# SiLU as one ScalarE function, a sum of weight blocks in place, and memory keys normalised from PSUM, in a four-layer decoder trunk

## The chip, the cores and the metric

The kernel runs on one core of a Trainium2 chip. The core has TensorE (PE; its weight loads are shown apart as PEld), VectorE (DVE), ScalarE (ACT), GpSimd (POOL) and SyncE (SP), which here issues DMAs. The metric is device time in microseconds of one execution of the whole kernel; less is better.

## What is computed

A decoder trunk of four layers over 256 tokens of width 1024, all in float32. Each layer is half a SwiGLU, a token mixer with a memory attention beside it, and another half SwiGLU:

```python
def swiglu(x, wg, wu, wd):
    return (jax.nn.silu(x @ wg) * (x @ wu)) @ wd          # d_ff = 2816

for i in range(4):
    h = rms_norm(x, ffn_norm[i, 0]); x = x + 0.5 * swiglu(h, ...)
    h = rms_norm(x, mix_norm[i])
    y_mix, q_mem = (retention, dsa, nsa)[i % 3](h)        # layers 0 and 3: retention
    y_mem = memory_attention(q_mem, mem, ...)
    x = x + concatenate([y_mix, y_mem]) @ w_out[i]
    h = rms_norm(x, ffn_norm[i, 1]); x = x + 0.5 * swiglu(h, ...)

def memory_attention(q_raw, mem, norm_g, w_kv, qn, kn):   # 256 memory tokens, 4 heads of 64
    k, v = split(rms_norm(mem, norm_g) @ w_kv)
    k = rms_norm(k per head, kn); q = rms_norm(q_raw per head, qn)
    return softmax(q @ k.T / 8) @ v
```

## The kernel before

The 256 tokens are two blocks `t` of 128. Weights come from HBM as units of two blocks of 1 MB (128 x 2048 floats), read in one order by SP's queue (`load`, line 184) into three buffers called `raw`; a load can go out only when its buffer has been read for the last time, and the loads keep their order.

**Split weights.** Each product is made as three matmuls, so each quarter of a unit (128 x 1024) is split first: ACT copies it into `hi` (type F32R), DVE subtracts that from the source into `lo` (lines 281, 282). There are nine buffers of each. `mm3` (lines 309 to 311) multiplies hi, lo and hi by the split activations `sh`, `sl`. The splits are handed out by `tick`, once or twice per projection of 24 matmuls (`project`).

**An FFN** (`ffn`) walks through eleven gate-and-up units and six units of down rows in the order FFN_ORDER. A gate-and-up projection gives a PSUM bank `pg` of 128 x 512 (256 gate, 256 up), from a ring of two banks shared with all other projections. Line 1265 takes tanh of half the gate on ACT, line 1266 makes (tanh + 1) times the gate on DVE, line 1271 multiplies by the up half and by the square of the row's norm factor r into `h`; the bank is free then. Two ticks later PE transposes h (line 1279), and ACT and DVE split the result (1280, 1281). Since this h holds twice the SiLU, line 1298 adds the down projection to x with 0.25. The factors r, r/2 (`rh`) and r*r (`r2`) come from `norm_stats` by four small POOL instructions.

**Joint units.** Gate-and-up units 4 with 5 and 8 with 9 of each FFN (16 joint units in all) are multiplied by a scheme with seven products in place of eight (`joint`, lines 491 to 493). It needs sums of weight blocks: `t1` = b12 + b11 comes by a load and an adding DMA on POOL's queue (line 229) into two tiles of the kind `sum` (a ring of nine tiles with the tag a4); `t2` and `t4` are made by DVE in place over t1 (line 250); `t3` is t1 minus b11 by DVE (line 247), into two more a4 tiles. Each of the seven is then split as above (lines 253, 254). The three other raw blocks b11, b22, b21 fill the three `raw` buffers; the buffer of b11 is the first to be free, and the first load of down rows behind the joint unit goes into it.

**The memory's keys** (`mem_kv`, twice per layer, for all four layers): a projection into `pmkv`; ACT copies the keys, scaled by the row's factor, into `mk0` and the values into V; POOL squares mk0, DVE sums per head, POOL makes the power -1/2 (`rsqrt`, lines 392 and 394) and multiplies mk0 by it; PE transposes the result (line 691) into `mkT`. The helper `head_sq` (line 554), used for queries, squares on ACT straight from PSUM and sums on DVE.

The order of each engine's instructions is not that of the code: the framework lays it out from dependencies and its own durations, per engine, except in the opening (`in_order`). Exp is used in the mixers alone (lines 601 and 1165), all of a block's mixer work being flushed ahead of its output projection.

Of the kernel before, what the change touches and what calls it, by code (L numbers as in the profile page):

```python
# [11 lines left out]
AF = mybir.ActivationFunctionType  # L12
OP = mybir.AluOpType
AX = mybir.AxisListType
# [66 lines left out]
class Net:  # L81
# [155 lines left out]
    def split_joint(self, u):  # L237
        nc = self.nc
        raw, parts = self.raw.pop(u), self.parts[u]
        parts.update({n: [] for n in ("b11", "t1", "t2", "t3", "b21", "t4", "b22")})  # L240
        half = lambda n, q: raw[n][:, 1024 * q:1024 * q + 1024] if n[0] == "b" else raw[n][q]

        def quarter(name, src, q, plus):
            x = half(src, q)
            if name == "t3":
                raw.setdefault("t3", []).append(self.t4([128, 1024], "sum"))
                nc.vector.tensor_sub(raw["t3"][q], x, half("b11", q))
                x = raw["t3"][q]
            elif plus:
                nc.vector.tensor_add(x, x, half(plus, q))  # L250
            hi = self.wp.tile([128, 1024], F32R, name="hi", tag="hi", bufs=HALVES)
            lo = self.wp.tile([128, 1024], F32R, name="lo", tag="lo", bufs=HALVES)
            nc.scalar.activation(hi, x, AF.Copy)  # L253
            nc.vector.tensor_sub(lo, x, hi.bitcast(F32))  # L254
            parts[name].append((hi, lo))

        for name, src, plus in (("b11", "b11", None), ("t1", "t1", None), ("t2", "t1", "b22"), ("t3", "t1", None),
                                ("b21", "b21", None), ("t4", "t1", "b21"), ("b22", "b22", None)):
            for q in range(2):
                self.splits.append((u, lambda name=name, src=src, q=q, plus=plus: quarter(name, src, q, plus)))  # L260
# [395 lines left out]
    def mem_kv(self, i, um, uw):  # L656
        nc = self.nc
        mh, ml = zip(*self.parts[um])
        kT = self.t2([128, 2, 256], "mkT")
        V = self.t2([128, 2, 4, 65], "mV")  # L660
        self.memkv[i] = kT, V
        nc.gpsimd.memset(V[:, :, :, 64:65], 1.0)

        class Stationary:
            def __init__(self, tiles, c):
                self.t, self.c = [x.rearrange("p (k m) -> p k m", k=4) for x in tiles], c

            def __getitem__(self, key):
                return self.t[key[1] // 4][:, key[1] % 4, self.c]

        for m in range(2):
            p = self.pB("pmkv")
            c = slice(m * 128, m * 128 + 128)
            self.project(p, (Stationary(mh, c), Stationary(ml, c)), uw)
            r = self.rmem[m]
            k0 = self.t1([128, 4, 64], "mk0")
            nc.scalar.activation(k0.rearrange("p h d -> p (h d)"), p[:, :256], AF.Copy, scale=r)
            nc.scalar.activation(V[:, m, :, :64], p[:, 256:].rearrange("p (h d) -> p h d", d=64),
                                 AF.Copy, scale=r)
            sq = self.t1([128, 4, 64], "mksq")  # L680
            nc.gpsimd.tensor_tensor(sq, k0, k0, op=OP.mult)
            ss = self.ts(4, "mss")
            nc.vector.tensor_reduce(ss, sq, axis=AX.X, op=OP.add)
            rk = self.rsqrt(ss, 4, 1.0 / 64, EPS, "mrk")
            k1 = self.t1([128, 4, 64], "mk1")
            nc.gpsimd.tensor_tensor(k1, k0, rk[:, :, None].to_broadcast([128, 4, 64]), op=OP.mult)

            def turn(k1=k1, c=c):
                pt = self.pC("pT")
                for j in range(2):  # L690
                    nc.tensor.transpose(pt[:, j], k1[:, 2 * j:2 * j + 2].rearrange("p h d -> p (h d)"), self.ident)
                nc.scalar.activation(kT[:, :, c], pt[:, :2], AF.Copy, scale=self.mqk[:, i:i + 1])

            self.later(WAIT["mkv"], turn, 2)
            self.tick()
# [548 lines left out]
    def ffn(self, t, g, st):  # L1244

        nc = self.nc
        H, acc, nd = {}, None, 0
        X = self.X[t]
        for kind, ui in FFN_ORDER:
            u = yield  # L1250
            if not H:
                s, r, rh, r2 = st["n"]
            if kind == "g":
                r_, rh_, r2_ = r, rh, r2
                if u == 0:
                    p = self.first[t]
                elif isinstance(u, tuple):
                    p, (_, r_, rh_, r2_) = u
                else:
                    p = self.pB("pg")  # L1260
                    self.project(p, s, u)
                if t and ui == 0:
                    self.sums()
                th = self.t1([128, 256], "th")
                nc.scalar.activation(th, p[:, :256], AF.Tanh, scale=rh_)  # L1265
                nc.vector.scalar_tensor_tensor(th, th, 1.0, p[:, :256], op0=OP.add, op1=OP.mult)  # L1266

                if ui % 2 == 0:
                    h = self.t2([128, 512], "h")
                hs = h[:, ui % 2 * 256:ui % 2 * 256 + 256]  # L1270
                nc.vector.scalar_tensor_tensor(hs, th, r2_, p[:, 256:], op0=OP.mult, op1=OP.mult)
                if ui % 2 or ui == 10:
                    n = 4 if ui % 2 else 2
                    hl = H[ui // 2] = [self.t2([128, 4, 128], f"hT{x}", F32R) for x in "hl"]

                    def turn(h=h, hl=hl, n=n):
                        c = self.pC("pT")
                        for k in range(n):
                            nc.tensor.transpose(c[:, k], h[:, k * 128:k * 128 + 128], self.ident)  # L1279
                        nc.scalar.activation(hl[0][:, :n], c[:, :n], AF.Copy)  # L1280
                        nc.vector.tensor_sub(hl[1][:, :n], c[:, :n], hl[0][:, :n].bitcast(F32))  # L1281

                    self.later(WAIT["h"], turn)
            else:
                pr = self.parts[u]
                if acc is None:
                    acc = self.pA("acc")
                nk = len(pr)
                for cb in range(2):
                    for k in range(nk):  # L1290
                        hl = H[ui]
                        wh, wl = pr[k]
                        o = cb * 512
                        self.mm3(acc[cb], hl[0][:, k], hl[1][:, k], wh[:, o:o + 512], wl[:, o:o + 512],
                                 nd == 0 and k == 0, nd == 5 and k == nk - 1)
                    if nd == 5:
                        xs = X[:, cb * 512:cb * 512 + 512]
                        nc.vector.scalar_tensor_tensor(xs, acc[cb], 0.25, xs, op0=OP.mult, op1=OP.add)
                        if g is None:
                            nc.scalar.dma_start(self.a["out"][t * 128:(t + 1) * 128, cb * 512:cb * 512 + 512], xs)  # L1300
                        else:
                            (self.norm_half if g >= 8 else self.norm_kept)(t, g, cb, st)
                    if cb == 0:
                        self.tick()
                nd += 1
        if g is not None:
            self.norm_stats(t, st)
# [303 lines left out]
```

## Time and profile before

| | us |
|---|---|
| median of 3 runs | 2041.11 (2036.3 to 2041.76) |
| the profiled execution, its own time | 2034.82 |
| its span, first to last instruction | 2033.0 |
| PE busy | 2004.1 (99%) |
| DVE busy | 1554.8 (76%) |
| ACT busy | 1114.5 (55%) |
| POOL busy | 198.5 (10%) |

The granted clock of TensorE is 0.998 of full speed over the span. In the page's groups and the lists by line, a row names line, engine, operation, output and inputs, shape and count, then busy microseconds in total, mean nanoseconds of one, idle time of that engine just before them and what ended it. Matmuls overlap: one shows 0.39 us although the next starts 0.23 us later.

### The profile page before, as it was taken

How to read it: one execution, taken by the hardware profiler on the slowest of the kernel's cores; microseconds unless marked ns; L12 is line 12 of the kernel's file. 1: busy time of each engine (PE TensorE's matmuls, PEld its weight loads, DVE VectorE, ACT ScalarE, POOL GpSimd, SP SyncE). 2: the span in 40 equal slices, each digit the busy share in tenths (PEclk: the TensorE clock that was granted, in tenths of full speed). 3: DMA queues.
4: the chain of work that ended last, by engine and by line, in shares of the span. 5: the costliest groups of instructions: out<-in, count | busy, mean ns of one | idle time of the engine just before them, and what ended most of it. 6: DMA issues, size and time to landing. Idle time of an engine off the chain costs nothing.

```text
span 2033.0 us, 25241 instructions
## 1 busy us (share of the span) xinstructions
PE 2004.1 (99%) x9486; PEld 1615.2 (79%) x9486; DVE 1554.8 (76%) x2241; ACT 1114.5 (55%) x1562; POOL 198.5 (10%) x317
## 2 busy tenths in 40 slices
PE   8999999999999999999999999999999999999999
PEld 6777777888888787888788788878888878778887
DVE  7877756888787787887788876668887878657875
ACT  5545555556555555655555554555555646545553
POOL 0000402000001022100000113220000000301000
PEclk9999999999999999999999999999999999999999
DMA  6656535565545533655556553135655566435553
GB/s 246 221 187 228 187 117 194 165 229 222 192 186 178 203 114 125 205 189 169 218 193 232 188 179 131 67 110 202 217 197 186 166 228 223 150 125 199 194 166 125
DMA packets 57770, 368.53 MB, mean 181 GB/s; under 512 B 6576, under 2 KB 6992, under 8 KB 18864
## 3 DMA queue, kind: packets, MB, share of 16 engines
q1 hardware_dynamic: 51696, 347.76, 46.3%
q0 software_dynamic: 4800, 17.19, 4.8%
q10 hardware_dynamic: 1152, 1.97, 0.3%
q8 instruction: 75, 1.23, 0.2%
q14 instruction: 47, 0.39, 0.1%
HBM read 365.84 MB, written 1.05 MB: 180 GB/s over the span
## 4 chain that ended last, share of the span: by engine, by line
PE 87%; DMA 5%; DVE 4%; ACT 1%; issue 1%; POOL 1%; SPq 0%; ACTq 0%; POOLq 0%; DVEq 0%
PE pg L309 8%; PE pg L311 8%; PE pg L310 8%; PE acc L310 8%; PE acc L311 8%; PE acc L309 8%; DMA sum<-gu 4%; PE pg L492 3%; PE pg L491 3%; PE pg L493 3%; PE p L309 3%; PE p L310 3%; PE p L311 3%; PE pT L1279 2%; PE pT L564 1%; PE po L309 1%
## 5 line engine op out<-in xcount | busy, mean ns | idle before, releaser
L282 DVE TENSOR_TENSOR lo<-raw,hi 128x1024 fp32r<-128x1024 f32 (+3 forms) x516 | 614.1, 1216 | 103.3 <-ACT hi L281 96.8
L281 ACT ACTIVATE hi<-raw 128x1024 fp32r<-128x1024 f32 (+3 forms) x516 | 527.3, 1046 | 187.0 <-PE pg L311 53.7
L309 PE MATMUL pg<-hi,sh 128*128 128x512 f32 x896 | 355.5, 397 | 4.5 <-ACT hi L1364 3.4
L310 PE MATMUL pg<-lo,sh 128*128 128x512 f32 x896 | 351.1, 392 | 0.7 <-DVE lo L1365 0.7
L311 PE MATMUL pg<-hi,sl 128*128 128x512 f32 x896 | 350.0, 391 | 0.0
L310 PE MATMUL acc<-lo,hTh 128*128 128x512 f32 x704 | 281.1, 403 | 0.5 <-DVE lo L282 0.3
L311 PE MATMUL acc<-hi,hTl 128*128 128x512 f32 x704 | 278.8, 400 | 0.0
L309 PE MATMUL acc<-hi,hTh 128*128 128x512 f32 x704 | 278.1, 399 | 0.0
L253 ACT ACTIVATE hi<-sum 128x1024 fp32r<-128x1024 f32 x128 | 132.3, 1058 | 166.8 <-PE acc L311 82.2
L309 PEld LDWEIGHTS pg<-hi,sh 128*128 128x128 f32 x896 | 168.5, 188 | 39.6 <-ACT hi L1364 4.8
L311 PEld LDWEIGHTS pg<-hi,sl 128*128 128x128 f32 x896 | 168.5, 188 | 35.5
L310 PEld LDWEIGHTS pg<-lo,sh 128*128 128x128 f32 x896 | 168.8, 188 | 35.1 <-DVE lo L1365 2.3
L254 DVE TENSOR_TENSOR lo<-sum,hi 128x1024 fp32r<-128x1024 f32 x128 | 154.4, 1227 | 42.0 <-ACT hi L253 39.9
L310 PEld LDWEIGHTS acc<-lo,hTh 128*128 128x128 f32 x704 | 132.7, 188 | 36.8 <-DVE lo L282 7.6
L1265 ACT ACTIVATE th<-pg,rh 128x256 f32<-128x256 f32 x128 | 60.3, 471 | 178.4 <-PE pg L311 173.0
L309 PEld LDWEIGHTS acc<-hi,hTh 128*128 128x128 f32 x704 | 132.9, 189 | 29.4 <-ACT hTh L1280 1.6
L311 PEld LDWEIGHTS acc<-hi,hTl 128*128 128x128 f32 x704 | 132.9, 189 | 26.1 <-DVE hTl L1281 0.2
L1266 DVE SCALAR_TENSOR_TENSOR th<-th,pg 128x256 f32<-128x256 f32 x128 | 53.5, 418 | 101.8 <-ACT th L1265 101.2
L254 DVE TENSOR_TENSOR lo<-raw,hi 128x1024 fp32r<-128x1024 f32 x96 | 114.6, 1223 | 16.5 <-ACT hi L253 16.3
L309 PE MATMUL p<-hi,sh 128*128 128x512 f32 (+4 forms) x320 | 125.2, 391 | 0.3 <-DVE dq_b L546 0.3
L311 PE MATMUL p<-hi,sl 128*128 128x512 f32 (+4 forms) x320 | 121.2, 379 | 0.0
L310 PE MATMUL p<-lo,sh 128*128 128x512 f32 (+4 forms) x320 | 120.9, 378 | 0.0
(345 smaller groups left out, 3180.1 us busy)
## 6 DMA issues: line engine op xcount, KB each, us to landing
raw<-gu SPq DMA_DIRECT2D x158, 1024.0 KB, 5.1
raw<-dn SPq DMA_DIRECT2D x88, 1024.0 KB, 4.8
raw<-ret SPq DMA_DIRECT2D x20, 1024.0 KB, 4.9
sum<-gu SPq DMA_DIRECT2D x32, 512.0 KB, 7.0
sum<-gu POOLq DMA_DIRECT2D x32, 512.0 KB, 9.5
raw<-wout SPq DMA_DIRECT2D x16, 1024.0 KB, 4.8
raw<-mkv SPq DMA_DIRECT2D x8, 1024.0 KB, 4.9
raw<-nsa SPq DMA_DIRECT2D x6, 1024.0 KB, 4.9
```

Source lines behind the costliest of these rows:

```text
L253: nc.scalar.activation(hi, x, AF.Copy)
L254: nc.vector.tensor_sub(lo, x, hi.bitcast(F32))
L281: nc.scalar.activation(hi, src, AF.Copy)
L282: nc.vector.tensor_sub(lo, src, hi.bitcast(F32))
L309: mm(out, ah, bh, start=start, stop=False)
L310: mm(out, ah, bl, start=False, stop=False)
L311: mm(out, al, bh, start=False, stop=stop)
L491: mm(bank, a[0][:, k], bh, start=first and k == 0, stop=False, skip_group_check=True)
L492: mm(bank, a[0][:, k], bl, start=False, stop=False, skip_group_check=True)
L493: mm(bank, a[1][:, k], bh, start=False, stop=k == 3, skip_group_check=True)
L1265: nc.scalar.activation(th, p[:, :256], AF.Tanh, scale=rh_)
L1266: nc.vector.scalar_tensor_tensor(th, th, 1.0, p[:, :256], op0=OP.add, op1=OP.mult)
```

## The change

Three edits. In the FFN, ACT's Tanh becomes Silu with the factor r, the DVE pass of line 1266 goes, the product with the up half takes r in place of r2, and x gets 0.5 in place of 0.25. In the joint units, t3 is written over the raw block b11 in place of two new tiles. In `mem_kv`, the scaled copy k0 goes; squares come from PSUM by `head_sq` on ACT; POOL multiplies the power by the row's factor (4 columns); and a DVE pass multiplies the keys from PSUM.

```diff
             if name == "t3":
-                raw.setdefault("t3", []).append(self.t4([128, 1024], "sum"))
-                nc.vector.tensor_sub(raw["t3"][q], x, half("b11", q))
-                x = raw["t3"][q]
+                nc.vector.tensor_sub(half("b11", q), x, half("b11", q))
+                x = half("b11", q)
...
             r = self.rmem[m]
-            k0 = self.t1([128, 4, 64], "mk0")
-            nc.scalar.activation(k0.rearrange("p h d -> p (h d)"), p[:, :256], AF.Copy, scale=r)
+
+            ss = self.head_sq(p[:, :256], 4, r, "mk")
             nc.scalar.activation(V[:, m, :, :64], p[:, 256:].rearrange("p (h d) -> p h d", d=64),
                                  AF.Copy, scale=r)
-            sq = self.t1([128, 4, 64], "mksq")
-            nc.gpsimd.tensor_tensor(sq, k0, k0, op=OP.mult)
-            ss = self.ts(4, "mss")
-            nc.vector.tensor_reduce(ss, sq, axis=AX.X, op=OP.add)
             rk = self.rsqrt(ss, 4, 1.0 / 64, EPS, "mrk")
+            rr = self.ts(4, "mrr")
+            nc.gpsimd.tensor_scalar(rr, rk, r, None, op0=OP.mult)
             k1 = self.t1([128, 4, 64], "mk1")
-            nc.gpsimd.tensor_tensor(k1, k0, rk[:, :, None].to_broadcast([128, 4, 64]), op=OP.mult)
+            nc.vector.tensor_mul(k1, p[:, :256].rearrange("p (h d) -> p h d", d=64),
+                                 rr[:, :, None].to_broadcast([128, 4, 64]))
...
-                nc.scalar.activation(th, p[:, :256], AF.Tanh, scale=rh_)
-                nc.vector.scalar_tensor_tensor(th, th, 1.0, p[:, :256], op0=OP.add, op1=OP.mult)
+                nc.scalar.activation(th, p[:, :256], AF.Silu, scale=r_)
...
-                nc.vector.scalar_tensor_tensor(hs, th, r2_, p[:, 256:], op0=OP.mult, op1=OP.mult)
+                nc.vector.scalar_tensor_tensor(hs, th, r_, p[:, 256:], op0=OP.mult, op1=OP.mult)
...
-                        nc.vector.scalar_tensor_tensor(xs, acc[cb], 0.25, xs, op0=OP.mult, op1=OP.add)
+                        nc.vector.scalar_tensor_tensor(xs, acc[cb], 0.5, xs, op0=OP.mult, op1=OP.add)
```

## Rows read from the trace of the kernel before

**Rows 1.** Page, part 1: busy time, share of the span, instructions of each engine.

```profile
PE 2004.1 (99%) x9486; PEld 1615.2 (79%) x9486; DVE 1554.8 (76%) x2241; ACT 1114.5 (55%) x1562; POOL 198.5 (10%) x317
```

**Rows 2.** Waits of PE: waiting line, releaser: us in total, times, longest.

```profile
PE pT L1279 <- DVE h L1271: 9.3, 6, 4.1
...
PE pT L691 <- POOL mk L686: 2.9, 3, 1.4
PE pT L564 <- ACT nsa_p L601: 2.0, 2, 1.2
```

**Rows 3.** Windows: stretch, us, busy of PE, PEld, DVE, ACT, POOL, clock, DMA.

```profile
69.96:73.37 3.41, 3.41 (x10) 2.68 (x9) 3.41 (x4) 3.01 (x6) 1.08 (x3) 0.50 0.00 0
73.40:100.00 26.60, 26.60 (x116) 21.47 (x115) 22.69 (x24) 15.96 (x18) 1.72 (x2) 1.00 0.50 180
```

**Rows 4.** Timeline at 940 us: start, us, instruction, [idle before, its releaser].

```profile
939.83 1.06 ACT L253 ACTIVATE hi<-sum 128x1024 fp32r<-128x1024 f32 x1 [2.22 <-DMA sum<-gu]
...
940.80 0.46 ACT L1265 ACTIVATE th<-pg,rh 128x256 f32<-128x256 f32 x1
...
941.29 0.42 DVE L1266 SCALAR_TENSOR_TENSOR th<-th,pg 128x256 f32<-128x256 f32 x1 [1.17 <-ACT th L1265]
...
941.63 1.22 DVE L254 TENSOR_TENSOR lo<-sum,hi 128x1024 fp32r<-128x1024 f32 x1
...
943.29 0.44 PE L1279 MATMUL pT<-ident,h 128*128 128x128 f32 x2 [0.84 <-DVE h L1271]
```

**Rows 5.** Timeline at 67 us, the longest wait for h.

```profile
67.71 0.41 DVE L1266 SCALAR_TENSOR_TENSOR th<-th,pg 128x256 f32<-128x256 f32 x1
...
69.71 0.49 PE L1279 MATMUL pT<-ident,h 128*128 128x128 f32 x2 [4.06 <-DVE h L1271]
```

**Rows 6.** Groups by line: shapes, count, busy us, mean ns, idle before.

```profile
L1265 ACT ACTIVATE th<-pg,rh 128x256 f32<-128x256 f32 x128 | 60.3, 471 | 178.4 <-PE pg L311 173.0 <-POOL rh L529 4.4
...
L1266 DVE SCALAR_TENSOR_TENSOR th<-th,pg 128x256 f32<-128x256 f32 x128 | 53.5, 418 | 101.8 <-ACT th L1265 101.2
...
L1266 DVE SCALAR_TENSOR_TENSOR th<-th,s 128x256 f32<-128x256 f32 x48 | 18.8, 419 | 0.0
...
L686 POOL TENSOR_TENSOR mk<-mk,mrk 128x256 f32<-128x256 f32 x8 | 7.0, 876 | 0.6
...
L681 POOL TENSOR_TENSOR mksq<-mk 128x256 f32<-128x256 f32 x8 | 6.2, 773 | 34.3 <-ACT mk L677 34.3
...
L847 POOL TENSOR_SCALAR nsc<-dq,rstd 128x6 f32<-128x6 f32 x4 | 1.6, 404 | 0.4
...
L1394 ACT ACT_TABLE_LOAD x1 | 1.3, 1283 | 5.6 <-DMA gains<-gains 5.6
```

**Rows 7.** Timeline of a joint unit at 395 us, and the page's row for down loads.

```profile
391.92 11.08 SPq L184 DMA_DIRECT2D raw<-dn  x2
...
394.57 3.50 DVE L254 TENSOR_TENSOR lo<-sum,hi 128x1024 fp32r<-128x1024 f32 x3 [1.58 <-ACT hi L253]
...
405.59 3.91 ACT L281 ACTIVATE hi<-raw 128x1024 fp32r<-128x1024 f32 x4
...
raw<-dn SPq DMA_DIRECT2D x88, 1024.0 KB, 4.8
```

**Rows 8.** Timeline in the NSA layer: its first Exp and PE behind it.

```profile
1252.41 1.85 ACT L601 ACTIVATE nsa_p<-nsa_s,nb,nsc 128x128 f32<-128x128 f32 x5 [1.82 <-DVE nb L598]
...
1252.92 0.33 PE L564 MATMUL pT<-ident,nsa_p 128*128 128x128 f32 x1 [0.81 <-ACT nsa_p L601]
```

**Rows 9.** Timeline of the opening: the first Tanh, and PE's wait for a bank.

```profile
25.84 0.47 ACT L1265 ACTIVATE th<-pg,rh 128x256 f32<-128x256 f32 x1 [0.34 <-POOL rh L529]
...
27.63 0.47 PE L309 MATMUL pg<-hi,sh 128*128 128x512 f32 x1 [1.05 <-DVE rb L445]
```

**Rows 10.** Timeline of ACT in the DSA layer, the first Exps.

```profile
729.37 1.93 ACT L601 ACTIVATE mem_p<-mem_s,nb,msc 128x256 f32<-128x256 f32 x4
```

**Rows 11.** Timeline of ACT at an FFN's first Tanh behind a mixer.

```profile
343.83 0.48 ACT L1265 ACTIVATE th<-pg,rh 128x256 f32<-128x256 f32 x1 [1.92 <-POOL rh L529]
```

## Prediction

> **What bounds the kernel now.** I read the busy time of each engine first: PE is busy for 2004.1 us, 99% of the span [rows 1]. A busy PE need not be at its peak, so I then read at what pace it goes: in the view by windows 116 matmuls, nearly all of 512 columns, take 26.60 us, 0.23 each, at full granted clock (2.4 GHz); ahead of that, 10 take 3.41 us at 0.50 of it (1.2 GHz) [rows 3]. So TensorE's own work sets the time, nothing in the diff changes that work, and the change can give back only what PE waits for. The next view is therefore the list of PE's waits [rows 2]. Two lines of it touch the edited code: transposes of h that wait for DVE (9.3 us in 6 waits, the longest 4.1, so the other five make 5.2, 1.04 each), and transposes of the memory's keys that wait for POOL (2.9 us in 3). Together 12.2 us: with the slow stretch behind the longest wait, that is nearly all that can be won. The profiled execution took 2034.82 us, 1.8 around its span; the median of the three runs shown is 2041.11, 6.3 more. I make the sum in microseconds on the profiled execution and put it on the median.
>
> **SiLU in one step.** It removes 128 and 48 passes of DVE over 128x256, 53.5 + 18.8 = 72.3 us of DVE's busy time [rows 6]. Almost all of that lies beside PE's work and is worth nothing; it counts where PE waits for h. The Silu itself stands where Tanh stood, with the same shape and a pointer scale; no row shows its price, so I take Tanh's 471 ns [rows 6] and hold less or more by a few tens of ns for nothing, since 176 of them spread over cover that PE does not see.
>
> Where PE waits for h, the cause is visible: ACT sits behind the arrival of a DMA-added sum (idle 2.22 us), converts it, and only then runs the Tanh; DVE runs the (th+1)*p pass at 941.29, puts a lo pass of 1.22 us between it and the product h, and PE, idle for 0.84 us, goes on at 943.29 [rows 4]. The DMA stays as late as it is. What goes is 0.42 us at the least (the pass itself) and at most the whole wait, if h moves into the place of the removed pass, ahead of that lo. I take the latter, since DVE chose the th pass at that moment, although the lo's hi had been made before th, and h needs then exactly what that pass needed. Five waits: between 5 x 0.42 = 2.1 and 5.2 us, taken 5.2. The sixth (4.1 us) has DVE's pass at 67.71 and PE's restart at 69.71 [rows 5]: with h (0.5 us) at 67.71 PE restarts near 68.2, 1.5 us earlier; at the least 0.42. Behind this wait TensorE runs at half clock: 10 matmuls take 3.41 us, against some 2.3 us at the pace of 0.23 us [rows 3]. That is 1.1 us; a wait of 2.6 us in place of 4.1 may or may not keep the clock up, so I take 0 and keep 1.1 for the range. Sum: -6.7, between -2.5 and -7.8.
>
> **Table loads.** The whole run before has one ACT_TABLE_LOAD of 1283 ns [rows 6], although Copy, Square, Tanh, Exp, Relu and Identity all run: these share a table set. Nothing in the trace shows whether Silu is with them, so the added loads are bounded by 0 and by one at each border between a stretch with Silu and a stretch with Exp: the borders of four mixers, both sides, and the first Silu, nine loads, 11.5 us of ACT. I take nine, and look at each border for cover. The one load itself ran only when ACT's wait of 5.6 us for a DMA was over [rows 6], so I let a load stand behind the wait of its ACTIVATE. In the NSA layer PE's first transposes stand right behind the first Exp, which waits for DVE, and PE is idle for 0.81 us [rows 8]: no cover, +1.28. In the opening PE waits 1.05 us for the PSUM bank that h frees [rows 9]; a load adds 1.28, the removed pass takes 0.42 out, and Silu no longer waits for rh behind rstd (0.34 us of idle): +0.5. At the other three mixers ACT has conversions queued behind the Exps [rows 10], PE is some us away: between 0 and 1.28 each, taken 0.35, so +1.05. At the four FFN starts behind a mixer the first Tanh already waits 1.92 us for POOL's rh [rows 11], Silu waits only for r, one POOL step sooner, and the other projection of 5 us is still ahead of PE: 0. Sum: +2.8, between 0 and +11.5.
>
> A rule that speaks against this part: the Trainium skill, "ScalarE: Activation LUTs" (What ACT_TABLE_LOAD costs), says that a switch to another set costs about 2.66 us, since some 1.38 us of draining come on top of the 1283 ns, and (Table sets: the hidden batching unit) that expensive functions each anchor a set of their own. The one load here agrees on the 1283; no run here shows a drain. By that rule nine switches would be an estimated 24 us of ACT, and with the cover above some 6 us of the path where I take 2.8.
>
> **The memory's keys.** Eight times (two blocks, four layers) the copy k0 goes (ACT, replaced by Square over the same PSUM block: even), POOL's squares go (773 ns each), POOL's product over 128x256 (876 ns) becomes a DVE pass from PSUM, for which I take the 418 ns of a DVE pass over the same shape with a PSUM operand, and POOL gets a product of 4 columns, priced by its product over 6 columns at 404 ns [rows 6]. The chain is shorter by 773 + 876 - 418 - 404 = 827 ns, if the new DVE pass finds DVE free; behind a lo it loses up to 1.22 us, so it can also be 0.4 us longer. PE waits for three of the eight. Taken -2.0 (the shortest of the three cannot give more than it has), between -2.9 and +1.2. What the change adds is a wait: DVE's pass stands in DVE's queue behind POOL's power and product, and the lo passes behind it stand with it, some 2 us, eight times. Today the reduce waits there for POOL's squares, which goes, so I count 0; if that cover is gone, lo passes are late for PE by up to 1 us each, +8. The PSUM bank is held until that pass, 3 us or more longer than the copy of V held it; the next project but one needs it 5.5 us later (24 matmuls of 0.23), so it stays free.
>
> **Third sum over b11.** The DVE pass is the same, and two buffers of the "sum" kind come free, for which no row read here waits. But the raw buffer of b11 is now read until the lo of t3's second half. Today the load of the next down rows goes out at 391.92, right when the subtraction has read b11; that lo ends at 394.57 + 3.50 = 398.07, so the load goes out 6.1 us later. It takes 4.8 us, lands at 402.9, and ACT reads it at 405.59; the second down load goes out at 391.92 + 11.08 - 0.33 = 402.67 as before [rows 7]. Cover left: 2.7 us. I count 0. All 16 joint units look like this.
>
> **Sum.** -6.7 + 2.8 - 2.0 = -5.9 us by the taken values; the DVE relief shortens also a few small waits that the list of PE's waits rounds away, for which I add 0.6 (estimate, a twentieth of the 12.2): -6.5. On the profiled execution 2028.3, on the median 2034.6 us. All ends together: -7.8 + 0 - 2.9 = -10.7, and -2.5 + 11.5 + 1.2 = +10.2.
>
> **Rivals.** (a) Little reaches PE: lo goes ahead of h as it does today, so the five waits give 2.1 and the sixth 0.4, the keys 0.8 and the loads cost 2.8: -0.5, 2040.6 us. For it: all six waits begin with a late DMA, which stays. (b) The loads find no cover: +11.5 in place of 2.8, so +2.2, 2043.3 us; against it, PE is seen to stand right behind an Exp in one mixer alone, and at the FFN starts the next product is already under way. By the skill's page, with a drain on top of each, it would end near an estimated 2056. (c) Slower: the b11 buffer. If t3's lo ends over 2.7 us later than I reckon, the down load comes late for ACT, the second one is queued behind it on SP, and each further us costs up to 1 us in each of 16 units. From 0.8 us past the cover (16 x 0.8 = 12.6, which eats the 6.5 and adds 6.1) it is slower by over 0.3%; at 1 us past, 2050.6 us. For it: in the code nothing holds that lo in its place; against it, all units show the same slack. (d) Each engine's order is laid out anew, since durations change: DVE's order already differs from ACT's [rows 4]. New waits in the mixers, of either sign, some 6 us: 2028 to 2047. (e) It doesn't do what it says: if Silu's set lacks Copy, each of 176 Silu brings two loads, 452 us of ACT, and the time would be over 2100.
>
> **How the numbers follow.** Forecast 0.50, (a) 0.20, (b) 0.09, (c) 0.07, (d) 0.12, (e) 0.02. A measurement of this kernel tells about 0.3%, 6.1 us, from no change. Of the forecast's own spread (-3 to -10) some three quarters lie beyond that; with half of (d), faster is 0.44; same takes the rest of the forecast, (a), most of (b) and a little of (d), 0.41; slower is (c), (e), and the rest of (b) and (d), 0.15. The range that leaves 2 in 10 out goes from 2026 (all gains, loads covered, and runs that lie 5.5 us apart) to 2046 (loads without cover, or new waits); the forecast's own is 2031 to 2038.
>
> **What would show it.** Right: line 1266's DVE groups gone, DVE's busy time down by some 70 us, the span down by under 0.5%; among PE's waits the one for h falls from 9.3 to under 4 and the one for the keys from 2.9 to about 1; ten ACT_TABLE_LOADs, the NSA layer's first transposes idle for about 2 us; the first down load some 6 us later in each joint unit, with PE's row there unchanged. Wrong: over ten loads, PE waits for lo of down rows in all 16 units, waits for PSUM banks near the memory projections, or an unchanged wait for h with DVE's lo still ahead of it.

## The result, and the profile of the changed kernel

The changed kernel takes 2025.06 us in the median (2022.19 to 2028.37), beside 2040.93 for the kernel before: a ratio of 0.9927, 95% interval 0.9904 to 0.995. Measured once more beside other kernels it gave 2024.35 and 0.9935 (0.9921 to 0.9949). So it is faster by 13 to 15 us. The forecast was 2034.6 with a range from 2026 to 2046; both medians lie 1 to 2 us below its low end; by the two ratios, on the 2041.11 that the forecast started from, they come to 2026.2 and 2027.8, just inside it. Either way the gain is about twice the 6.5 us forecast. On the profiled executions the distance is smaller, 2026.89 against 2034.82, 7.9 us, where the sum said 6.5. How 7.9 and 13 to 15 go together is the main question of the experiments.

The page of the changed kernel, part 1 (busy time, share, instructions):

```profile
PE 2002.0 (99%) x9486; PEld 1618.7 (80%) x9486; DVE 1490.5 (74%) x2073; ACT 1129.0 (56%) x1571; POOL 187.8 (9%) x309
```

Its list of PE's waits (us in total, times, longest):

```profile
PE pT L1276 <- DVE h L1268: 4.3, 3, 3.4
...
PE p L308 <- DVE dq_b L545: 1.3, 1, 1.3
...
PE pg L308 <- DVE h L1268: 1.1, 1, 1.1
...
PE pT L689 <- DVE mk L683: 0.8, 1, 0.8
```

DVE lost 64.3 us of busy time [rows 1]. PE does the same 9486 matmuls; the span is 7.9 us shorter and PE's busy time 2.1, so 5.8 of the 7.9 is idle time of PE. The wait for h fell from 9.3 us in 6 to 4.3 in 3, the one for the keys from 2.9 in 3 to 0.8 in 1 [rows 2]. The wait of `p` for DVE's `dq_b` was 0.3 and is 1.3; that of `pg` for h stands where the opening's wait for `rb` stood [rows 9].

The joint unit of [rows 4] now looks like this (timeline: start, us, instruction, [idle before, its releaser]):

```profile
935.48 1.06 ACT L252 ACTIVATE hi<-sum 128x1024 fp32r<-128x1024 f32 x1 [1.11 <-DMA sum<-gu]
...
936.45 0.45 ACT L1263 ACTIVATE th<-pg,rstd 128x256 f32<-128x256 f32 x1
...
936.93 0.48 DVE L1268 SCALAR_TENSOR_TENSOR h<-th,rstd,pg 128x256 f32<-128x256 f32 x1
...
937.33 2.35 DVE L253 TENSOR_TENSOR lo<-sum,hi 128x1024 fp32r<-128x1024 f32 x2
...
938.60 0.60 PE L1276 MATMUL pT<-ident,h 128*128 128x128 f32 x4
```

h stands where the removed pass stood, ahead of lo, and PE makes the transposes without idle time. The sum came less late here than in [rows 4] too: ACT stood for 1.11 us before it, where it had been 2.22. At the longest wait the DMA is late as before, and PE still stands for 3.42 us, with a half-clock stretch behind it. The timeline, and then the view by windows (PE, PEld, DVE, ACT, POOL busy, granted clock, DMA):

```profile
67.85 1.06 ACT L252 ACTIVATE hi<-sum 128x1024 fp32r<-128x1024 f32 x1 [3.44 <-DMA sum<-gu]
...
69.30 0.48 DVE L1268 SCALAR_TENSOR_TENSOR h<-th,rstd,pg 128x256 f32<-128x256 f32 x1 [2.38 <-ACT th L1263]
...
69.84 0.44 PE L1276 MATMUL pT<-ident,h 128*128 128x128 f32 x2 [3.42 <-DVE h L1268]
```

```profile
70.90:74.30 3.40, 3.40 (x10) 2.63 (x9) 3.40 (x5) 1.96 (x5) 2.79 (x3) 0.50 0.00 0
```

The table loads in the groups by line (count, busy us, mean ns, idle before), and then three of them in ACT's timeline: the opening, a mixer whose Exp waits (NSA) and one whose Exp doesn't (DSA):

```profile
L1263 ACT ACT_TABLE_LOAD x5 | 6.4, 1283 | 7.2 <-PE pg L310 7.2
L600 ACT ACT_TABLE_LOAD x4 | 5.1, 1283 | 4.7 <-DVE nb L597 4.7
```

```profile
25.29 0.19 ACT L525 ACTIVATION_READ_ACCUMULATOR scr<-x 128x1 f32 x1
25.49 1.28 ACT L1263 ACT_TABLE_LOAD   x1
26.79 0.47 ACT L1263 ACTIVATE th<-pg,rstd 128x256 f32<-128x256 f32 x1
...
1245.47 1.28 ACT L600 ACT_TABLE_LOAD   x1 [1.80 <-DVE nb L597]
1246.76 4.29 ACT L600 ACTIVATE nsa_p<-nsa_s,nb,nsc 128x128 f32<-128x128 f32 x12
...
724.53 0.85 ACT L280 ACTIVATE hi<-raw 128x768 fp32r<-128x768 f32 x1 [5.22 <-PE p L310]
725.39 1.28 ACT L600 ACT_TABLE_LOAD   x1
726.69 1.93 ACT L600 ACTIVATE mem_p<-mem_s,nb,msc 128x256 f32<-128x256 f32 x4
```

Nine loads in these two groups and one in the opening make ten, the number forecast, at the places forecast, each behind the wait of its ACTIVATE where there is one. The ACTIVATE before a load ends where the load starts (25.48 and 25.49 us), and the next starts 1.29 to 1.30 us after that: no drain shows on either side. So the 1.38 us that the Trainium skill adds for it ("ScalarE: Activation LUTs", What ACT_TABLE_LOAD costs) isn't there in this kernel, and the measurement decides.

### The profile page after: what moved, and what is told of

Same layout as the page of the kernel before. It is cut to its first block, busy times and chain, and to the rows that moved or that the text cites. A ratio compares the mean times of both kernels' runs of the same rounds, so it can differ in the third digit from the quotient of the medians.

```text
span 2025.1 us, 24989 instructions
## 1 busy us (share of the span) xinstructions
PE 2002.0 (99%) x9486; PEld 1618.7 (80%) x9486; DVE 1490.5 (74%) x2073; ACT 1129.0 (56%) x1571; POOL 187.8 (9%) x309
## 4 chain that ended last, share of the span: by engine, by line
PE 92%; DVE 2%; DMA 2%; ACT 1%; issue 1%; POOL 1%; SPq 0%; ACTq 0%; DVEq 0%; POOLq 0%
PE pg L310 9%; PE pg L308 9%; PE pg L309 9%; PE acc L309 8%; PE acc L308 8%; PE acc L310 8%; PE pg L491 3%; PE pg L490 3%; PE pg L492 3%; PE p L308 3%; PE p L309 3%; PE p L310 3%; PE pT L1276 2%; PE pT L563 1%; PE po L308 1%; PE pj L491 1%
## 5 line engine op out<-in xcount | busy, mean ns | idle before, releaser
L252 ACT ACTIVATE hi<-sum 128x1024 fp32r<-128x1024 f32 x96 | 102.0, 1062 | 163.0 <-PE acc L310 91.2
L253 DVE TENSOR_TENSOR lo<-raw,hi 128x1024 fp32r<-128x1024 f32 x128 | 151.3, 1224 | 27.1 <-ACT hi L252 26.9
L1263 ACT ACTIVATE th<-pg,rstd 128x256 f32<-128x256 f32 x128 | 60.3, 471 | 172.5 <-PE pg L310 172.3
L253 DVE TENSOR_TENSOR lo<-sum,hi 128x1024 fp32r<-128x1024 f32 x96 | 115.9, 1221 | 43.6 <-ACT hi L252 41.6
L1268 DVE SCALAR_TENSOR_TENSOR h<-th,rstd,pg 128x256 f32<-128x256 f32 x128 | 60.9, 475 | 115.4 <-ACT th L1263 115.2
L252 ACT ACTIVATE hi<-raw 128x1024 fp32r<-128x1024 f32 x128 | 127.9, 1047 | 20.6 <-PE pg L310 13.7
```

Of the source, the lines that this page charges most:

```text
L1263: nc.scalar.activation(th, p[:, :256], AF.Silu, scale=r_)
L1268: nc.vector.scalar_tensor_tensor(hs, th, r_, p[:, 256:], op0=OP.mult, op1=OP.mult)
```

## The experiments

All ratios are to the kernel before, run on the same chip, with 95% intervals; 0.001 is 2.04 us.

**The parts alone.** First SiLU on the kernel before:

```diff
-nc.scalar.activation(th, p[:, :256], AF.Tanh, scale=rh_)
-nc.vector.scalar_tensor_tensor(th, th, 1.0, p[:, :256], op0=OP.add, op1=OP.mult)
+nc.scalar.activation(th, p[:, :256], AF.Silu, scale=r_)
```

> Before with the SiLU edit alone. Theory A (the gain is the waits for h, less the table loads): five waits of about 1 us at 136, 885 to 951, 1127, 1670 and 1960 us go, the wait at 66 us loses 0.7, the loads give back 1 to 2.8; so 3 to 5 us below the kernel before, ratio 0.9975 to 0.9985, about half of what the whole change gave on the medians (15.9). Theory B (DVE's 72 us of relief is worth more than the waits in the list): nearly all of it is here, 10 us or more, ratio below 0.995. Ten ACT_TABLE_LOADs by both.

Measured: 2028.07 us, ratio 0.9944 (0.9924 to 0.9964), 11.4 us by the ratio (7.3 to 15.5 by its interval); ten loads. Theory A's size falls: this part alone gives twice what it allowed. It isn't yet theory B, since the relief need not lie in waits that A left out; that is what the later runs are for. The trace shows less of it than the median: its execution, 2032.43 us, was the slowest of the six, 2.4 us below the profiled one before. PE's waits for h, and one of them in the timeline:

```profile
PE pT L1278 <- DVE h L1270: 6.5, 5, 3.6
```

```profile
1124.10 1.06 ACT L253 ACTIVATE hi<-sum 128x1024 fp32r<-128x1024 f32 x1 [3.44 <-DMA sum<-gu]
...
1125.55 0.48 DVE L1270 SCALAR_TENSOR_TENSOR h<-th,rstd,pg 128x256 f32<-128x256 f32 x1 [2.40 <-ACT th L1265]
...
1126.09 0.44 PE L1278 MATMUL pT<-ident,h 128*128 128x128 f32 x2 [1.06 <-DVE h L1270]
```

Four of the five waits of about 1 us are gone, and two of 0.7 and 1.0 us have come at other places. This one stays although h goes ahead of lo, since the sum came so late that ACT stood for 3.44 us; the longest is still 3.6. So the removed pass helps only as far as the DMA lets it.

Then the third sum over b11:

```diff
-raw.setdefault("t3", []).append(self.t4([128, 1024], "sum"))
-nc.vector.tensor_sub(raw["t3"][q], x, half("b11", q))
-x = raw["t3"][q]
+nc.vector.tensor_sub(half("b11", q), x, half("b11", q))
+x = half("b11", q)
```

> Before with the third sum over b11 alone. Theory A (the 2.7 us of cover hold, as in the prediction): 0, within 1 us of the kernel before, ratio 0.9995 to 1.0005; the first load of down rows goes out about 6 us later in each of 16 joint units, and no wait for down rows is in PE's list. Theory B (two buffers fewer of the sum kind let the sums of the next joint unit start earlier, or DVE's new order in the joint units takes waits away): 2 to 5 us faster, ratio 0.9975 to 0.999, with fewer or shorter waits for h.

Measured: 2037.51 us, ratio 0.9993 (0.9976 to 1.001): nothing that can be told from no change. In the changed kernel the loads of the down rows stand like this in SP's queue and ACT's:

```profile
394.77 4.91 SPq L184 DMA_DIRECT2D raw<-dn  x2
...
402.27 3.98 ACT L280 ACTIVATE hi<-raw 128x1024 fp32r<-128x1024 f32 x4
```

The first load goes out 7.50 us ahead of ACT's reading (394.77 to 402.27), where before it was 13.67 (391.92 to 405.59 in [rows 7]): 6.2 us later, as forecast. With 4.8 us for the transfer 2.7 us of cover are left, and ACT reads the four halves without idle time. Over the whole kernel ACT waits for down rows for 1.7 us in 5, before it was 1.0 in 3, and PE's list has no wait that follows from it.

Then the memory's keys:

```diff
-nc.scalar.activation(k0.rearrange("p h d -> p (h d)"), p[:, :256], AF.Copy, scale=r)
+ss = self.head_sq(p[:, :256], 4, r, "mk")
...
-nc.gpsimd.tensor_tensor(sq, k0, k0, op=OP.mult)
...
+nc.gpsimd.tensor_scalar(rr, rk, r, None, op0=OP.mult)
-nc.gpsimd.tensor_tensor(k1, k0, rk[:, :, None].to_broadcast([128, 4, 64]), op=OP.mult)
+nc.vector.tensor_mul(k1, p[:, :256].rearrange("p (h d) -> p h d", d=64),
+                     rr[:, :, None].to_broadcast([128, 4, 64]))
```

> Before with the memory's keys alone. Theory A (the prediction): PE's three waits for the keys, 2.9 us together, fall to about 0.8, so 2.0 us faster, ratio 0.999. Theory B (the new DVE pass stands behind lo passes, or holds its PSUM bank for longer): 0 or up to 1.2 us slower, with a wait of PE for a bank that the DVE pass of the keys frees.

Measured: 2035.62 us, ratio 0.9986 (0.9974 to 0.9997), 2.9 us. Theory A. Of this run, PE's waits for h and for the keys, and then the group of the new DVE pass:

```profile
PE pT L1277 <- DVE h L1269: 11.8, 7, 5.4
...
PE pT L689 <- DVE mk L683: 0.9, 2, 0.7
```

```profile
L683 DVE TENSOR_TENSOR mk<-pmkv,mrr 128x256 f32<-128x256 f32 x8 | 3.4, 425 | 11.1 <-POOL mrr L681 11.1
```

The wait for the keys goes from 2.9 to 0.9. DVE does stand for POOL, 11.1 us in eight, but PE's list has the same wait for lo of later units as before (0.3 us in 2, at `acc`), so no lo behind it is late. The three ratios multiply to 0.9923, the whole change gave 0.9927 and 0.9935: the parts add up within the noise, and SiLU is about three quarters.

**What the table loads cost.** The changed kernel with Tanh in the place of Silu:

```diff
-nc.scalar.activation(th, p[:, :256], AF.Silu, scale=r_)
+nc.scalar.activation(th, p[:, :256], AF.Tanh, scale=r_)
```

> After with Tanh in place of Silu: as many instructions, but one table set for all, so that the nine added loads go; the gate is computed wrongly by that. Theory A (the prediction's bill for the loads): 2.8 us faster than after: 1.28 in the NSA layer, 0.5 in the opening, 1.05 in the other mixers, 0 at the FFN starts; ratio to before about 0.9915. Theory B (the loads are covered, since the layout moves projection matmuls ahead of the transposes that wait for Exp; the NSA layer's first transposes waited 0.43 us in after, 0.81 in before): 0.5 to 1 us faster than after, all of it in the opening; ratio about 0.9925. Theory C (a load costs more than its 1283 ns, by draining): more than 5 us faster.

Measured, in a kernel that leaves the SiLU out: 2020.82 us, ratio 0.9917 (0.9894 to 0.9939), 2.0 to 3.7 us below the two measurements of the changed kernel. Theory C falls. A and B can't be told apart by this time alone, but by PE's timeline in the NSA layer of the changed kernel:

```profile
1244.13 1.05 PE L589 MATMUL nsa_s<-nkT,dqT 64*128 64x128 f32 x13
...
1246.50 0.34 PE L309 MATMUL p<-lo,sh 128*128 128x384 f32 x1
1247.27 0.33 PE L563 MATMUL pT<-ident,nsa_p 128*128 128x128 f32 x1 [0.43 <-ACT nsa_p L600]
...
1257.32 0.41 PE L308 MATMUL p<-hi,sh 128*128 128x384 f32 x1 [1.26 <-DVE dq_b L545]
```

Before, the transposes of nsa_p stood right behind the scores and waited 0.81 us [rows 8]. Now eight projection matmuls stand between them, so the load is hidden there and the wait is 0.43. But 10 us later the next projection waits 1.26 us for a PSUM bank; before and in the Tanh run this wait is 0.3. It is 1.3 in all six traces in which a load stands ahead of that first Exp, and 0.3 in the eight others. Both theories had half of it: the layout did move matmuls, and the cost came back at another place.

**Loads that run early.** Two kinds of one-column activations in the changed kernel:

```diff
 nc.vector.memset(self.neghalf, -0.5)
+nc.scalar.activation(self.ts(1, "tbl"), self.neghalf[:, :1], AF.Silu)
...
 ops = {}
+if t == 1:
+    nc.scalar.activation(self.ts(1, "tbl"), st["n"][1], AF.Exp)
```

> After with two kinds of one-column activations added: a Silu at the start of the opening, and an Exp behind the norm ahead of each mixer, so that the tables are loaded while ACT waits for something else. Theory A (the bill of the Tanh run, about 2 us between 0.9927 and 0.9917, is the loads in the opening and ahead of the first Exps): ratio 0.9915 or a little less, 2 to 3 us below after; in the opening the first ACTIVATE starts 1.28 us earlier, at 5.7 us, if nothing else holds it; the matmul that waits 1.3 us for a PSUM bank in the NSA layer, which the Tanh run lacks, goes. Theory B (the differing layout, not the loads, made the Tanh run faster): within 1 us of after.

Measured: 2020.63 us, ratio 0.9918 (0.9905 to 0.9931). Theory A. ACT in the opening:

```profile
2.62 1.28 ACT L1346 ACT_TABLE_LOAD   x1 [2.62 <-issue]
...
6.09 0.37 ACT L1392 ACTIVATE sh<-pT,gains 128x128 fp32r<-128x128 f32 x1 [1.98 <-PE pT L1373]
```

The first ACTIVATE of the split starts at 6.09 in place of 7.00, held by PE's transpose and not by a table. The load at 25.49 is gone (nine loads in all, in place of ten), and PE's wait for dq_b is 0.3 again.

**The DVE pass put back.** The changed kernel with a pass of the same shape between Silu and h:

```diff
 nc.scalar.activation(th, p[:, :256], AF.Silu, scale=r_)
+nc.vector.scalar_tensor_tensor(th, th, 1.0, th, op0=OP.mult, op1=OP.max)
```

> After with a DVE pass over 128x256 put back between Silu and the product with the up half (it compares th with itself and leaves it as it is). Theory A (what the SiLU edit gives is the place of that pass on the way from ACT to h): the waits of about 1 us for h in the joint units come back, and with them 6 to 12 us over after, ratio to before 0.996 to 0.9985; the lo pass stands between it and h again. Theory B (the gain comes from Silu taking r in place of rh and r2, or from the other parts): within 2 us of after, ratio about 0.993.

Measured: 2040.45 us, ratio 1.0021 (1.0008 to 1.0033), some 18 us over the changed kernel. Its waits for h, and then DVE in the joint unit at 940 us:

```profile
PE pT L1277 <- DVE h L1269: 11.6, 8, 3.4
```

```profile
941.05 0.42 DVE L1264 SCALAR_TENSOR_TENSOR th<-th 128x256 f32<-128x256 f32 x1 [1.93 <-ACT th L1263]
941.39 1.22 DVE L253 TENSOR_TENSOR lo<-sum,hi 128x1024 fp32r<-128x1024 f32 x1
942.53 0.48 DVE L1269 SCALAR_TENSOR_TENSOR h<-th,rstd,pg 128x256 f32<-128x256 f32 x1
```

Theory A in its mechanism: with the pass, lo stands ahead of h again and the waits for h are back. In size it is above the 6 to 12 us that A gave. Of the 18 us, 11.4 are what SiLU alone gave and 2 to 4 the loads, which stay; the last 2 to 6 us are not explained by any line that I found. The profiled execution, 2036.45 us, is the fastest of the twelve, so what the others waited for is in no trace.

**Why the DMA is late at 66 us.** First the memory tokens' loads moved back:

```diff
-    nc.sync.dma_start(memx[m], a["mem"][m * 128:(m + 1) * 128])
+    self.load(memx[m], a["mem"][m * 128:(m + 1) * 128])
...
 if n == 5:
     constants_in()
+if n == 8:
+    memx_in()
```

> After with the two loads of the memory tokens (512 KB each) moved four loads back in SP's queue, behind units that the first FFN needs later. Theory A (the long wait for h at 66 us, 3.4 us in after and 4.1 in before, is bandwidth: the adding DMAs of the first joint unit share the DMA engines with these loads, 1 MB at some 350 GB/s being 2.9 us): the wait falls below 1 us and the half-clock stretch of 3.4 us at 71 us goes, so 3 to 5 us below after, ratio about 0.991. Theory B (the adding DMAs take their 12 to 14 us whatever else is under way): no change.

Measured: 2024.17 us, ratio 0.9938 (0.9926 to 0.9949), the changed kernel's own time. Theory A falls: the second adding DMA goes out at 51.54 and ACT takes its sum at 65.72, 14.2 us later; with the tokens' loads beside it, it was 14.5 (53.33 and 67.85).

```profile
51.54 0.87 POOL L229 DMA_DIRECT2D sum<-gu  x1 [0.24 <-issue]
...
65.72 1.06 ACT L252 ACTIVATE hi<-sum 128x1024 fp32r<-128x1024 f32 x1 [3.42 <-DMA sum<-gu]
```

This clears the tokens' loads, not bandwidth: the three raw blocks are still loaded beside the sums, and the DMA engines are as busy without the tokens (a share of 1.03 from 56 to 60 us and 1.01 from 60 to 64) as with them (1.02 and 1.06). No run takes those three away.

With the early table loads as well:

> After with the early table loads and with the memory tokens later, both. If both theories A hold and the two don't touch each other, 5 to 8 us below after, ratio 0.989 to 0.9905; if the opening's earlier start only makes the first joint unit wait longer for its sums, the sum of the two is less by up to 1.5 us than the two alone.

Measured: 2021.71 us, ratio 0.9922 (0.9911 to 0.9934): 0.0016 below the run before it, what the table loads give, and nothing from the tokens.

**The sums earlier.** What was left as a cause is when the adding DMAs can start. They follow the loads of `t1`, which stood in SP's queue behind two loads of down rows that wait for a raw buffer. In these runs the sums of a joint unit go out ahead of those two:

```diff
+if u + 1 < len(self.units) and self.units[u + 1][0] == "j":
+    self.fetch_sum(u + 1)
 self.raw[u] = []
 for ap in self.units[u][1]:
...
+def fetch_sum(self, u):
...
+    start("t1")
+    add("t1", b11)
```

On the kernel before, with Tanh and its DVE pass:

> The kernel before, with Tanh and its DVE pass, but with the sums' loads early. Theory A (the removed DVE pass counts only where the adding DMA is late): the waits for h, 9.3 to 11.8 us in the kernel before and its two variants with the old SiLU, fall below 5 us, and the kernel is 5 to 9 us faster than before, ratio 0.9955 to 0.9975. Theory B (the pass is late for reasons of DVE's own queue, the DMA being a mere companion): the waits for h of about 1 us stay and the ratio is above 0.9985.

Measured: 2025.7 us, ratio 0.9944 (0.9926 to 0.9963): what SiLU alone gives, and 2 us more than theory A's upper end. What ACT's conversions of a joint unit waited for, in the kernel before and then in this one (idle us, times), and the wait for h that is left in this one's list (a second one is 0.3):

```profile
  DMA sum<-gu: 18.1, 9
```

```profile
  PE pg L319: 22.6, 46
  issue: 4.2, 1
  DMA raw<-gu: 0.6, 1
```

```profile
PE pg L317 <- DVE h L1279: 2.0, 1, 2.0
```

No conversion waits for a sum any more, and transposes wait for h for 0.3 us in all, although the DVE pass and the lo ahead of h are still there:

```profile
934.14 0.41 DVE L1274 SCALAR_TENSOR_TENSOR th<-th,pg 128x256 f32<-128x256 f32 x1
934.47 1.22 DVE L262 TENSOR_TENSOR lo<-sum,hi 128x1024 fp32r<-128x1024 f32 x1
935.61 0.47 DVE L1279 SCALAR_TENSOR_TENSOR h<-th,r,pg 128x256 f32<-128x256 f32 x1
```

The wait for h had two causes in one chain, a late DMA and a pass that lets lo in. Without the late DMA it is gone but for 0.3 us; without the pass most of the waits of about 1 us go, and the longest stays as long as the sum is late.

On the changed kernel the early sums find little left to take:

> After with the loads and adding DMAs of each joint unit's sum put ahead of the two down rows before it in the queue of loads; same work, same buffers. Theory A (what is left of the waits for h is the adding DMA landing late behind 3 MB of other loads): the wait at 66 us falls from 3.4 to under 1 us, the half-clock stretch behind it goes, and the kernel is 3 to 5 us below after, ratio about 0.9905. Theory B (the adding DMAs stretch with whatever shares the DMA engines, or the down rows come late in their place): within 1 us of after, or slower, with waits of ACT for raw<-dn.

Measured: 2023.19 us, ratio 0.9926 (0.9914 to 0.9939). In time it is theory B, within 1 to 2 us of the changed kernel; in mechanism it is half of A: the wait at 66 us is gone, and another of 1.7 us at 60 us has come. Theory B's sign came too: ACT waits for down rows for 19.6 us, where the changed kernel has 1.7, though PE's list shows nothing of that.

```profile
ACT hi L288 <- DMA raw<-dn: 19.6, 10, 5.2
```

And the changed kernel, measured beside it, had little left at 66 us:

> The changed kernel once more, beside the three others of this call: ratio to before 0.9915 to 0.9935, with waits for h of 3 to 5 us in PE's list and ten table loads. If the first four executions were lucky (the parts alone gave 0.9944, 0.9993 and 0.9986, whose product is 0.9923), it lies above 0.994.

Measured: 0.9935, as given above. Its profiled execution took 2022.4 us, with a wait for h of 1.90 us in place of 3.42 and no half-clock stretch behind it (PE in the timeline, then the window that begins 2 us later):

```profile
65.93 0.44 PE L1276 MATMUL pT<-ident,h 128*128 128x128 f32 x2 [1.90 <-DVE h L1268]
```

```profile
68.00:71.40 3.40, 3.40 (x16) 2.74 (x16) 2.43 (x4) 2.11 (x5) 2.10 (x4) 1.00 0.00 1
```

The last run has early sums and early tables on the changed kernel:

> The same with the early table loads as well: 2 us below the run with the early sums alone (what the Tanh run and the preload run gave against after), ratio 0.9895 under theory A, 0.992 under theory B of that run.

Measured: 2020.96 us, ratio 0.9916 (0.9902 to 0.993), 2.0 us below the run with early sums alone. This and the run with the early tables alone (0.9918) are the lowest times of the kernels that leave nothing out, some 2 to 4 us below the changed kernel; their intervals overlap with its own. Two pairs of runs on the same chip differ in the early loads alone and agree in the sign (0.0016 with the tokens later, 0.0010 with the early sums). A third comparison, 0.0020, is of the early tables with the run of the later tokens, so it differs in the tokens too and shares a run with the first pair.

## Where the prediction was right and where it wasn't

**The bound.** Right: PE's work is the same to 2 us, and the rest of what moved is its waits.

**SiLU.** This is the step that failed, in its size. The term was -6.7 without the loads, -3.9 with the 2.8 for them. The part alone gave 11.4 us with them (7.3 to 15.5), so 13 to 15 without. The mechanism is borne out: h stands in the slot of the removed pass, and with the pass put back the waits return. It was not borne out in full, since "the DMA stays as late as it is" left waits that the removed pass doesn't end (1.06 at 1126 us in the run with SiLU alone). The base was too small: all durations came from one execution, and it was a light one. Two profiles with the same SiLU code, those of the runs with the third sum alone and the keys alone, have 11.5 and 11.8 us of waits for h where [rows 2] have 9.3, and 5.0 and 5.4 for the longest where [rows 5] have 4.1. At that longest wait the clock is at half for 6.80 us in the keys' run, with PE at work in 4.58 of them, against 3.41 in [rows 3]:

```profile
67.32:74.12 6.80, 4.58 (x12) 3.71 (x13) 6.80 (x9) 3.73 (x6) 1.96 (x3) 0.50 0.08 34
```

The prediction took 0 for the clock and kept 1.1 for the range, and that was read too low: the ten matmuls of [rows 3] include two transposes and one that had begun before. The others start 0.43 us apart (70.43, 70.86, 71.28 us), 0.20 more than at full clock, so an estimated 1.6 us are lost in 3.41. The 0.6 for waits that the list rounds away is neither shown nor refuted: gaps of 0.04 to 0.25 us between matmuls, over what is usual for a pair of these shapes, sum to 52.1 us before and 48.9 after. With the pairs sorted by tiles as well the difference is 0.8 in place of 3.2, and matmuls at half clock are among them.

**The sum put on the median.** The prediction took what separates the profiled execution from the others over to the changed kernel, 6.3 us by three executions. Over all 56 of the record the kernel before has a median of 2037.65, 2.8 above the profiled 2034.82; only eight are faster. The changed kernel's nine executions lie between 2022.19 and 2028.37 with a median of 2024.35, 2.5 below its profiled one. So one profile was light and the other heavy, and 7.9 with 2.8 and 2.5 makes the 13.3 us between the medians: that the forecast was good on the profiled executions (2028.3 against 2026.89) was in part luck. What made the other executions of the kernel before longer may well be the wait that the change removes, as the two profiles with 11.5 and 11.8 us suggest. No trace of the others shows it, so this is argued and not shown.

**Table loads.** Number, places and position behind the wait were right. The bill of 2.8 us is held by the runs: the Tanh run gives 2.0 to 3.7, the two pairs with and without early loads 3.3 and 2.0, in which some 0.8 to 0.9 us belong to the opening's own load, that the kernel before had on its path too (ACT's first ACTIVATE at 6.85 there and 7.00 in the changed kernel, against 6.09). Where it falls was half wrong: in the NSA layer I counted 1.28 at the first transposes, and it is 1.26 at a bank 10 us later. That is rival (d), the order laid out anew, inside the forecast. In the opening, where I had +0.5, the first function starts 0.95 later (26.79 against 25.84 in [rows 9]) and PE goes on 0.20 later (27.83 against 27.63); but the function starts at 26.19 and 24.36 in the two runs with the old SiLU, so one execution can't settle half a microsecond there. The FFN starts cost nothing that PE sees.

**The keys.** -2.0 forecast, 2.9 measured with an interval from 0.6 to 5.3. POOL's product of 4 columns takes 0.30 us where I took 0.404 from one of 6 [rows 6]; DVE's pass takes 425 ns for the 418 taken. DVE's wait for POOL, put at some 2 us each, is 1.4 (11.1 in 8), and the cover held.

**Third sum over b11.** 0 forecast, 0.9993 measured. The load goes out as late as reckoned, and rival (c) didn't come. (Its 16 x 0.8 is 12.8, not 12.6, which changes nothing.)

**Rivals.** (a) is refuted by the row at 936.93, h ahead of lo. For it I had named that all waits begin with a late DMA, which stays; the run with the early sums shows that this was the other half of the same wait. (b) and (e) did not come, nor a drain.

**Left open:** how much of SiLU's 11.4 us lies in waits for h in the executions without a trace, 2 to 6 us of the run with the pass put back, and why one execution waits 3.4 us at 66 us and another 1.9 with the same order of work.

## What to carry to other kernels

A wait that ends with a chain of two engines and a DMA can be shortened at any of its links; before counting two remedies, ask whether they take the same wait. Where a wait hangs on a DMA's arrival, one profile shows one draw of it: read the longest wait and the clock behind it in two or three executions before putting a sum on the median. Nine more table loads cost 2 to 4 of 2024 us here, and one-column activations, placed ahead of the Exp that PE waits for, took 2 to 3 of that out.

## What the runs showed of the hardware that was not expected

Silu ran beside Copy and Square without further loads; only the borders to Exp cost one, 1283 ns each, and the price stayed at that.

The half clock (1.2 GHz) is not only the companion of an idle PE. In the profiled execution of the run with the early tables PE went at half the clock for 23.90 us, behind 11.70 us in which it was never idle (windows):

```profile
1265.00:1276.70 11.70, 11.70 (x96) 10.79 (x95) 7.92 (x26) 5.46 (x10) 2.59 (x4) 1.00 0.01 2
1276.70:1300.60 23.90, 23.90 (x92) 19.70 (x92) 12.47 (x33) 9.08 (x20) 5.54 (x10) 0.50 0.26 88
```

That execution took 2032.7 us, the five others of the same kernel 2018.69 to 2023.08. The early tables are not what it takes: six other executions, two of the kernel before and four of other variants, have a granted clock of 0.990 to 0.993 over the span as well and lie 9.6 to 11.3 us above their kernels' medians, though no trace of them is kept. A short stretch of the same kind stands in the changed kernel's own profile, behind 13.55 us in which PE was never idle:

```profile
1323.55:1326.96 3.41, 3.41 (x13) 2.82 (x12) 2.44 (x10) 2.51 (x4) 1.36 (x1) 0.50 0.21 26
```

No run here shows what set either off.

In the first joint unit the second adding DMA of 512 KB took 14.2 to 14.5 us from issue to its reader, with the tokens' loads beside it or without; over all 32 of a kernel the median from issue to landing is 9.9 us in the changed kernel and 8.9 with the sums early. Starting it earlier took the wait for it away; taking 1 MB of other loads away didn't.
